# Neighbourhood attention in a two-layer diffusion trunk: turning the context keys' and context queries' probabilities by DMA instead of on TensorE, with half-precision values

## The chip, the cores and the metric

One core of one Trainium2 chip runs the whole program. The metric is device microseconds of one execution (us); lower is better. A core has five engines with a queue each: TensorE (PE, matmuls and transposes), VectorE (DVE), ScalarE (ACT), GpSimd (POOL) and SyncE (SP, which here only issues DMAs). Each engine takes its own instructions strictly in order.

## What is computed

Two layers of a trunk with 512 latent tokens (an 8 x 64 grid) and 256 context tokens, width 1024, 8 heads of 64. Each layer has two token mixers in parallel; the change touches the first, neighbourhood attention (below "NA"); the second is grouped-query attention ("GQ").

```python
s_win = einsum('bchd,bicjhd->bhcij', qr, kw) * scale + bias      # an 8 x 16 window of latent keys
s_ctx = einsum('bchd,blhd->bhcl', qr, kc) * scale                # all 256 context keys
p = softmax(concatenate([s_win, s_ctx]))
out = einsum(p_win, vw) + einsum(p_ctx, vc)                      # for the latent queries
c_a_att = _attend(cqa, cka, cva)      # layer 0 only: context queries read the context keys
```

The latent order is grid column by grid column, so that the window of 128 queries lies in 256 consecutive keys.

## The kernel before

**Stages.** Each layer runs one after the other: projections of K, V and Q for NA (line 433 to 435 are the three matmuls of every projection: a high and a low part of the activation against a high and a low part of the weight, each in fp32r), then the NA stage, then the projections of GQ, the GQ stage, and the merge with the output projection. While an attention stage runs, `pipeline` hands TensorE pieces of other projections as filling (the gates and z paths, tiles `psf` and `psx`), so that it has work while probabilities are made. Their weights come over SP's queue as `raw`, are rounded on ACT (`whi`) and the rest is taken on POOL or DVE (`wlo`).

**One head of the NA stage.** `na_scores` makes four tiles of 128 queries x 512 scores: for tile 0 the two edge groups of 64 queries, for tiles 1 to 3 128 inner queries; columns 0 to 255 are neighbours, columns 256 to 511 the 256 context keys. For each tile TensorE makes the scores in PSUM (`pss`); DVE adds the bias and takes the maximum (line 958, `p<-pss,bint` or `bedg`); ACT takes the exponential with its row sum (line 961); DVE inverts the sum (line 762); then the tile is multiplied with it, on DVE (line 765) for tiles 0 and 2 and on POOL (lines 767 and 768) for tiles 1 and 3 (`NA_POOL`). In layer 0 `ctx_scores` adds one tile for the 256 context queries.

`na_values` comes one head later (`pipeline` calls the scores of head h before the values of head h - 1). A value matmul needs the probabilities with the keys on the partitions, so each 128 x 128 block is turned first: `transpose_split` transposes four blocks on TensorE into one PSUM tile (`pst`, lines 777 and 779), ACT rounds it to fp32r (`pth`, line 785), DVE takes the rest (`ptl`, line 786). There are four such groups per head: two for the context keys (`k` = 0, 1: eight transposes, then lines 981 and 982 with 512 columns) and two for the neighbours (eight transposes, then lines 986 to 992 with 192 and 256 columns). In layer 0 `ctx_values` has one more group of four for the context queries (lines 905 and 906, 256 columns). The values themselves are four 64-column pieces per head (high, low, low, high, in fp32r), so that one matmul gives the product with the high part in one half of the partitions and the one with the low part in the other; `head_out` adds the halves and multiplies with the z path.

**GQ already turns by DMA.** There `turned` (lines 799 to 804) rounds the probabilities to fp16 on ACT (`h`, line 802), takes the rest in fp16 on POOL or DVE (line 803) and issues one `dma_start_transpose` on SP's queue (line 804), 12 blocks of 128 x 128 for a tile of 768 keys. Its values are fp16 pairs, scaled by one factor so that they fit.

**What sets the order.** The program is written head by head; a scheduler then places each engine's instructions, so an engine's queue can hold instructions of two heads and of filling mixed. Tiles come from pools with a fixed number of buffers: eight `p` (seven in layer 0), two `pth` and two `ptl`, three `raw`, eight `whi` and `wlo`, one `bint` and one `bedg` for the bias of a head. In layer 0 half of the adaLN gate's dot products (`gate_steps((0,), ...)`: line 295 on DVE, 16 of them, with eight weight tiles `rawb`) is spread over heads 4 to 7 of the NA stage.

Of the kernel before, what the change touches and what calls it, by code (L numbers as in the profile page):

```python
# [7 lines left out]
F32 = mybir.dt.float32  # L8
# [17 lines left out]
NP_NA = (7, 8)  # L26
# [3 lines left out]
NT_NA = 2  # L30
P_LOG = 9.7
V_UP = 2.0 ** 14
NA_POOL = (1, 3)
# [37 lines left out]
def hybrid_kernel(es: ExitStack, tc, x, ctx, cvec, w_ada, w_ada0, small, gvec, w_in, w_o_a, w_o_b, w_out,  # L71
# [482 lines left out]
    def split_v(ps, hi, lo, hi_src=None):  # L554
        S.copy(R(hi), ps)
        V.tensor_tensor(R(lo), ps, hi, ALU.subtract)

    def evac_va(dsts):
        def f(t, ps):
            d = dsts[t // 3].rearrange("p (t n) -> p t n", t=3)[:, t % 3, :]  # L560
            d = d.rearrange("p (r q d) -> p r q d", q=4, d=64)
            s = ps.rearrange("p (r e d) -> p r e d", e=2, d=64)
            hi, lo = d[:, :, 0:4:3, :], d[:, :, 1:3, :]
            split_v(s, hi, lo)
        return f
# [18 lines left out]
    def layer(l, hx, nxt, start):  # L584
# [144 lines left out]
        va = [big("va0"), big("va1")]  # L729
        w = load_w(W, C_AV, 512, KT, mix_lo)  # L730
        for t in range(6):
            tok_proj(w, 512, a_hx, t, evac_va(va))
            if first:
                if t == 0:
                    for ts in AKG[1:]:
                        evac_ak(ts)
                hp["lag"] = max(2, hp["lag"] - (t > 0))
            if t > 2:
                run(bg, per_bg)
# [9 lines left out]
        for t in range(qt):  # L749
            tok_proj(w, 512, a_hx, t, evac_na(qav, True, gq, YB if first else 4))  # L750
            run(bg, per_bg)
# [7 lines left out]
        if True:  # L759
            def softmax_tail(p, n, r, pieces, eng=None):  # L760

                V.reciprocal(r, r)
                for i, (c0, c1) in enumerate(pieces):
                    if eng is None:
                        V.tensor_scalar(p[:, c0:c1], p[:, c0:c1], r[:, i:i + 1], 0.5, ALU.mult, ALU.mult)
                    else:
                        G.tensor_scalar(r[:, i:i + 1], r[:, i:i + 1], 0.5, None, ALU.mult)
                        G.tensor_tensor(p[:, c0:c1], p[:, c0:c1],
                                        r[:, i:i + 1].to_broadcast([128, c1 - c0]), ALU.mult)

            def transpose_split(blocks, n0=0, n1=512):
# [8 lines left out]
                if att["spare"]:  # L780
                    hi, lo = R(p_tile()[:, 0:512]), R(p_tile()[:, 0:512])
                else:
                    hi = att["p"].tile([128, 512], F32R, tag="pth", name=nm("pth"), bufs=att["nt"])
                    lo = att["p"].tile([128, 512], F32R, tag="ptl", name=nm("ptl"), bufs=att["nt"])
                S.copy(hi[:, n0:n1], pt[:, n0:n1])
                V.tensor_tensor(lo[:, n0:n1], pt[:, n0:n1], F(hi[:, n0:n1]), ALU.subtract)
                return hi, lo

            def head_out(po, e, dst, eng=None):
# [5 lines left out]
                S.copy(a, po[o:o + 64, :n])  # L795
                V.tensor_tensor(a, po[m:m + 64, :n], a, ALU.add)
                (eng or G).tensor_tensor(dst, dst, a, ALU.mult)

            def turned(p, n, out, eng):

                h = att["p"].tile([128, 2, n], F16, tag="h", name=nm("h"), bufs=att["nh"])
                S.copy(h[:, 0], p[:, :n])  # L802
                eng.tensor_tensor(h[:, 1], p[:, :n], h[:, 0], ALU.subtract)  # L803
                nc.sync.dma_start_transpose(out, h.rearrange("p a n -> p (a n)"))
# [9 lines left out]

            def shrink(v, s, mx, row):

                V.tensor_reduce(mx[:, 0:1], v, AX, ALU.max)
                V.tensor_reduce(mx[:, 1:2], v, AX, ALU.min, negate=True)
                V.tensor_tensor(mx[:, 0:1], mx[:, 0:1], mx[:, 1:2], ALU.max)
                pt = psw(512, "t")  # L820
                T.transpose(pt[0:1, 0:128], mx[:, 0:1], ident)
                V.tensor_reduce(row[:, 0:1], pt[0:1, 0:128], AX, ALU.max)
                T.matmul(pt[:, 128:129], row[:, 0:1].to_broadcast([1, 128]), ident[0:1, 0:1], start=True, stop=True)
                V.tensor_scalar(s[:, 1:2], pt[:, 128:129], 1.0e-30, 1.0 / V_UP, ALU.max, ALU.mult)
                V.reciprocal(s[:, 0:1], s[:, 1:2])
                V.tensor_scalar(s[:, 1:2], s[:, 1:2], 0.5, None, ALU.mult)
# [40 lines left out]
            def ctx_scores(q, kh, kl, ct=None):  # L867
# [7 lines left out]
                if ct is not None:  # L875
# [6 lines left out]
                if ct is not None:  # L882
                    turned(p, 512, ct.rearrange("p a i k n -> p (a i k) n"), G)
                    return ct, r
                softmax_tail(p, 512, r, [(0, 256), (256, 512)])
                return p

            def ctx_values(p, vsl, dst, e, back=None):
                if back is not None:
                    ct, r = p  # L890
                    ps = psw(512, "v")
                    po = ps[:, 0:256]
                    divide(ps[:, 256:512], r, e, dst, back)
                    for k in range(2):
                        for a in range(2):
                            T.matmul(po.rearrange("p (i n) -> p i n", i=2), vsl(4 + k), ct[:, a, :, k, :],
                                     start=k + a == 0, stop=k + a == 2)
                    head_out(po, e, dst)
                    return
                hi, lo = transpose_split(  # L900
# [599 lines left out]
```

## Time and profile before

| what | us |
|---|---|
| median of 3 runs (1125.44 to 1126.06) | 1125.91 |
| the profiled execution | 1127.56 |
| its span, first to last instruction | 1125.6 |
| NA stage of layer 0, from the span's start | 149.5 to 305.2 |
| NA stage of layer 1 | 771.4 to 881.7 |
| GQ stage of layer 0 | 382 to 550 |
| GQ stage of layer 1 | 938 to 1061 |

The stages' limits are read from the first and last matmul of their lines. In a row of groups, "x35 | 19.7, 585" means 35 instructions, 19.7 us of busy time in all, 585 ns for one on average; what follows the second bar is the time that the engine was idle just before them, and who ended it. Matmuls are pipelined: the time of one reaches from its start to the end of its result, while the next has started long before. What one costs is therefore read from the distance of two starts in the timeline, not from its own duration.

### The profile page before, as it was taken

Reading aid. Unit: us, or ns where it says so; the run is one execution under the profiler, and the core shown is the slowest. Engines: PE = TensorE matmul, PEld = TensorE weight load, DVE = VectorE, ACT = ScalarE, POOL = GpSimd, SP = SyncE. Lnnn points to the kernel's source line nnn. Section 1 sums busy time; section 2 is a strip of 40 time slices with the busy share of each in tenths; the row PEclk is TensorE's granted clock in tenths of the full one; section 3 lists DMA queues with packets and bytes.
Section 4 is the critical chain, followed back from the end, with each engine's and each line's share of the span. In section 5 each row is a group of like instructions: output and inputs, shape, how many; then the busy total and the mean of one; then the engine's idle time right before and its main releaser. Section 6 shows DMA issues by size and latency. Waiting matters only on the chain.

```text
span 1125.6 us, 16862 instructions
## 1 busy us (share of the span) xinstructions
PE 1093.3 (97%) x5826; PEld 905.3 (80%) x5826; DVE 774.7 (69%) x1492; ACT 579.0 (51%) x1154; POOL 490.6 (44%) x405
## 2 busy tenths in 40 slices
PE   8999999999999999979999999999999999999998
PEld 5688888888998877757788888888888987776677
DVE  4666788897466477776577785458878765677473
ACT  6453266665433576755330284326666446776431
POOL 1054254654247144454521545235554563563531
PEclk9999999999999999989999999999999999999999
DMA  9454322242351488869633532553333236989742
GB/s 373 143 172 140 114 63 66 73 136 89 93 168 38 123 201 185 185 172 269 173 108 125 183 129 72 142 174 92 100 107 116 59 105 172 188 224 239 197 145 80
DMA packets 192222, 161.29 MB, mean 143 GB/s; under 512 B 116364, under 2 KB 158088, under 8 KB 190472
## 3 DMA queue, kind: packets, MB, share of 16 engines
q1 hardware_dynamic: 184800, 145.82, 46.8%
q0 software_dynamic: 2368, 7.87, 2.1%
q10 hardware_dynamic: 4968, 6.53, 1.7%
q8 instruction: 46, 0.75, 0.3%
q14 instruction: 40, 0.33, 0.1%
HBM read 115.58 MB, written 17.32 MB: 118 GB/s over the span
## 4 chain that ended last, share of the span: by engine, by line
PE 38%; issue 4%; DVE 3%; DMA 3%; POOL 2%; ACT 1%; SPq 1%; POOLq 0%; ACTq 0%
PE psx L435 6%; PE psx L433 6%; PE psx L434 6%; PE psf L433 4%; PE psf L434 4%; PE psf L435 4%; PE pss L955 1%; PE pss L861 1%; POOL wlo L406 1%; PE pss L862 1%; PE pst L779 1%; PE pst L1148 1%; DMA raw<-in_w_o_a_dram 1%; PE pst L1149 1%; DMA raw<-in_w_in_dram 1%
## 5 line engine op out<-in xcount | busy, mean ns | idle before, releaser
L420 POOL TENSOR_TENSOR wlo<-raw,whi 128x512 fp32r<-128x512 f32 x70 | 97.9, 1405 | 106.1 <-ACT whi L418 70.4
L433 PE MATMUL psf<-hx,whi 128*128 128x512 f32 (+1 forms) x360 | 138.0, 383 | 3.2 <-ACT zt L614 2.4
L435 PE MATMUL psf<-hx,wlo 128*128 128x512 f32 (+1 forms) x360 | 135.8, 377 | 0.0
L434 PE MATMUL psf<-hx,whi 128*128 128x512 f32 (+1 forms) x360 | 135.1, 375 | 0.0
L433 PE MATMUL psx<-whi,hx 128*128 128x512 f32 (+1 forms) x328 | 120.8, 372 | 0.0
L434 PE MATMUL psx<-wlo,hx 128*128 128x512 f32 (+1 forms) x328 | 119.6, 366 | 0.0
L435 PE MATMUL psx<-whi,hx 128*128 128x512 f32 (+1 forms) x328 | 119.5, 365 | 0.0
L418 ACT CAST whi<-raw 128x512 fp32r<-128x512 f32 x136 | 82.3, 620 | 64.0 <-DMA raw<-in_w_in_dram 35.3
L406 POOL TENSOR_TENSOR wlo<-raw,whi 128x512 fp32r<-128x512 f32 x40 | 61.2, 1535 | 122.1 <-ACT whi L403 80.1
L803 POOL TENSOR_TENSOR h<-p,h 128x768 f16<-128x768 f32 (+1 forms) x40 | 65.7, 1644 | 96.4 <-ACT h L802 72.0
L403 ACT CAST whi<-raw 128x512 fp32r<-128x512 f32 x88 | 54.1, 623 | 99.2 <-PE psx L435 34.2
L420 DVE TENSOR_TENSOR wlo<-raw,whi 128x512 fp32r<-128x512 f32 x66 | 73.6, 1115 | 30.6 <-ACT whi L418 29.0
L504 POOL TENSOR_TENSOR ss<-ss,ehalf 128x8 f32<-128x8 f32 (+2 forms) x40 | 62.5, 1566 | 72.9 <-DVE ss L501 72.8
L433 PEld LDWEIGHTS psf<-hx,whi 128*128 128x128 f32 x360 | 67.9, 188 | 15.4 <-ACT zt L614 3.7
L435 PEld LDWEIGHTS psf<-hx,wlo 128*128 128x128 f32 x360 | 67.8, 188 | 11.6
L1131 DVE CUSTOM_DVE_ANT_0 p<-pss,vb 128x768 f32<-128x768 f32 x64 | 60.3, 953 | 23.6 <-PE pss L862 21.1
L434 PEld LDWEIGHTS psf<-hx,whi 128*128 128x128 f32 x360 | 67.9, 189 | 10.3
L1132 ACT ACTIVATE p<-pss,mx 128x768 f32<-128x768 f32 x64 | 57.6, 900 | 34.7 <-DVE mx L1131 33.7
L435 PEld LDWEIGHTS psx<-whi,hx 128*128 128x128 f32 x328 | 61.9, 189 | 10.0
L434 PEld LDWEIGHTS psx<-wlo,hx 128*128 128x128 f32 x328 | 62.0, 189 | 9.2
L433 PEld LDWEIGHTS psx<-whi,hx 128*128 128x128 f32 x328 | 61.8, 189 | 8.9
L435 PE MATMUL psx<-hx,wlo 128*128 128x256 f32 (+1 forms) x208 | 68.0, 327 | 0.0
(362 smaller groups left out, 3095.8 us busy)
## 6 DMA issues: line engine op xcount, KB each, us to landing
raw<-in_w_in_dram SPq DMA_DIRECT2D x168, 256.0 KB, 2.9
rawb<-in_w_ada_dram SPq DMA_DIRECT2D x48, 256.0 KB, 2.8
raw<-in_w_out_dram SPq DMA_DIRECT2D x32, 256.0 KB, 2.9
tg<-gs SPq DMA_DIRECT2D x4, 1536.0 KB, 6.8
rawx<-in_w_ada_dram SPq DMA_DIRECT2D x4, 1024.0 KB, 9.8
rawy<-in_w_ada_dram SPq DMA_DIRECT2D x4, 1024.0 KB, 9.5
gs<-zt ACTq DMA_DIRECT2D x16, 256.0 KB, 2.0
raw<-in_w_o_a_dram SPq DMA_DIRECT2D x16, 256.0 KB, 3.4
```

What stands on the lines that cost most here:

```text
L403: S.copy(hi[:, :n], raw[:, :n])
L406: e.tensor_tensor(lo[:, :n], raw[:, :n], F(hi[:, :n]), ALU.subtract)
L418: S.copy(hi, raw)
L420: lo_eng(i).tensor_tensor(lo, raw, F(hi), ALU.subtract)
L433: T.matmul(ps, lhs[0], rhs[0], start=first, stop=False)
L434: T.matmul(ps, lhs[0], rhs[1], start=False, stop=False)
L435: T.matmul(ps, lhs[1], rhs[0], start=False, stop=last)
L504: G.tensor_tensor(ss, ss, ehalf[:, :n], ALU.pow)
L779: T.transpose(pt[:, c0:c0 + 128], src, ident)
L803: eng.tensor_tensor(h[:, 1], p[:, :n], h[:, 0], ALU.subtract)
L1131: V.tensor_tensor_reduce(p, pss, lift, -1.0, 3e38, ALU.add, ALU.min, mx[:, 0:1])
L1132: S.activation(p, pss, AF.Exp, bias=mx[:, 0:1], accum_out=r[:, i:i + 1])
```

## The change

1. **Context keys.** In `na_scores` columns 256 to 511 of each of the four tiles go through `turned`: ACT rounds 128 x 256 to fp16, POOL takes the rest, and DMA transposes on SP's queue put four blocks into `ht`, a tile in SBUF (two halves, used by even and odd heads). Tile 0 is split over two DMAs of 64 queries, because its halves belong at both ends of the 512 queries. `na_values` reads `ht` directly; the two groups of TensorE transposes with their ACT and DVE passes go.
2. **Context queries** (layer 0): the tile of 128 x 512 goes the same way with one DMA of eight blocks; one group of transposes goes.
3. **Neighbours** stay with `transpose_split`, but its two parts are now fp16.
4. **Values** of NA become fp16 pairs: each token tile is copied out, `size` takes its absolute maximum (ACT and DVE), `split_va` finds one factor for all (`shrink`: one transpose, one one-column matmul) and `halves` makes high and low. The probabilities are lifted by 2^14 (`P_UP`), `head_out` takes the factor back. GQ's values use the same helpers, with two pieces instead of three.
5. **Multiplication with the inverse sum** for tiles 1 and 3: on ACT instead of POOL (`NA_ACT`).
6. **Gate dots** of half 0: from NA of layer 0 to the projections of GQ of layer 0.
7. **Buffers**: eight `p` in both layers, four `h`, one `hc`; `pth` and `ptl` become one fp16 tile `pt`.

```diff
-NA_POOL = (1, 3)
+NA_ACT = (1, 3)
+P_UP = 2.0 ** 14
...
+            if t == 0:
+                split_va()
...
-                    if eng is None:
-                        V.tensor_scalar(p[:, c0:c1], p[:, c0:c1], r[:, i:i + 1], 0.5, ALU.mult, ALU.mult)
+                    if on_act:
+                        S.activation(p[:, c0:c1], p[:, c0:c1], AF.Copy, scale=r[:, i:i + 1])
                     else:
-                        G.tensor_scalar(r[:, i:i + 1], r[:, i:i + 1], 0.5, None, ALU.mult)
-                        G.tensor_tensor(p[:, c0:c1], p[:, c0:c1],
-                                        r[:, i:i + 1].to_broadcast([128, c1 - c0]), ALU.mult)
+                        V.tensor_scalar(p[:, c0:c1], p[:, c0:c1], r[:, i:i + 1], P_UP, ALU.mult, ALU.mult)
...
-                nc.sync.dma_start_transpose(out, h.rearrange("p a n -> p (a n)"))
+                for o, n0, n1 in out:
+                    nc.sync.dma_start_transpose(o, h[n0:n1].rearrange("p a n -> p (a n)"))
...
-                    softmax_tail(p, 512, r[:, 0:1], [(0, 512)], G if i in NA_POOL else None)
+                    softmax_tail(p, 512, r[:, 0:1], [(0, 512)], i in NA_ACT)
+                    at = [(0, 64, 0), (448, 512, 64)] if i == 0 else [(128 * i - 64, 128 * i + 64, 0)]
+                    turned(p[:, 256:512], 256, [(ht[:, :, a:b], n, n + b - a) for a, b, n in at], G)
...
                 for k in range(2):
-                    c0 = 256 + 128 * k
-                    hi, lo = transpose_split(
-                        [(pe[:, c0:c0 + 128], None)]
-                        + [(pp[:, c0:c0 + 128], 64 + 128 * i) for i, pp in enumerate((p0, p1, p2))])
-                    T.matmul(po, vsl(4 + k), hi, start=k == 0, stop=False)
-                    T.matmul(po, vsl(4 + k), lo, start=False, stop=False)
+                    for a in range(2):
+                        T.matmul(po, vsl(4 + k), ht[:, 2 * a + k, :], start=k + a == 0, stop=False)
...
-            bg = gate_steps((0,), att["p"]) if first else []
+            bg = []
...
-            bg = []
+            bg = gate_steps((0,), hp["p"]) if first else []
```

**TensorE, NA of layer 1.** Before, this stands in TensorE's queue around the values of head 4 (`psv_8685`) and the context keys of head 5 (`pst_8844` and `pst_8855`, each four transposes of tiles `p`):

```order
L991 MATMUL psv_8685<-ptl_8727,va_1485_7303 128x256
L992 MATMUL psv_8685<-ptl_8727,va_1486_7304 128x192
L777 MATMUL pst_8844<-ident,p_8646 128x2x64
L779 MATMUL pst_8844<-ident,p_8656 128x128
L779 MATMUL pst_8844<-ident,p_8667 128x128
L779 MATMUL pst_8844<-ident,p_8677 128x128
L777 MATMUL pst_8855<-ident,p_8646 128x2x64
L779 MATMUL pst_8855<-ident,p_8656 128x128
L779 MATMUL pst_8855<-ident,p_8667 128x128
L779 MATMUL pst_8855<-ident,p_8677 128x128
L955 MATMUL pss_8969<-kh_7883,qs_8951 128x512
```

In the changed kernel, the values of head 4 (`psv_8687`) read the context keys' probabilities from `ht` with no transposes ahead of them; these rows are the last of their four matmuls and the first of the neighbours' (`pt`), each weight load a row of its own:

```order
L996 LDWEIGHTS va_7261
L996 MATMUL psv_8687<-ht_7859,va_7261 128x512
L1000 LDWEIGHTS va_7261
L1000 MATMUL psv_8687<-pt_8697,va_7261 128x192
L1001 LDWEIGHTS va_7261
L1001 MATMUL psv_8687<-pt_8697,va_7261 128x256
```

Eight transposes per head have left this queue; what the matmuls wait for is now a DMA's landing instead of ACT's and DVE's passes over a PSUM tile.

**SP, NA of layer 1.** Before, SP's queue holds the weights of the filling (`raw`), the bias of each head (`bint`, `bedg`) and stores of the z path (`zs`, `gs`):

```order
L618 DMA gs_83<-zt_8787 128x512
L415 DMA raw_8942<-in_w_in_dram 128x2x256
L935 DMA bedg_7875<-in_bias_edge_dram 64x128 x2
L415 DMA raw_9245<-in_w_in_dram 128x2x256
L618 DMA gs_83<-zt_8921 128x512
L415 DMA raw_9251<-in_w_in_dram 128x2x256
```

In the changed kernel, halfway through the stage, the turns of heads 3 and 4 (`h_8366` is the last tile of head 3, `h_8477` to `h_8522` are head 4's) stand between them:

```order
L840 DMA_TRANSPOSE ht_7859<-h_8366 128x4x128
L840 DMA_TRANSPOSE ht_7859<-h_8477 128x4x64 x2
L840 DMA_TRANSPOSE ht_7859<-h_8493 128x4x128
L840 DMA_TRANSPOSE ht_7859<-h_8507 128x4x128
L947 DMA bint_7853<-in_bias_int_dram 128x256
L417 DMA raw_8921<-in_w_in_dram 128x2x256
L417 DMA raw_9201<-in_w_in_dram 128x2x256
L417 DMA raw_9207<-in_w_in_dram 128x2x256
L949 DMA bedg_7854<-in_bias_edge_dram 64x128
L840 DMA_TRANSPOSE ht_7859<-h_8522 128x4x128
```

The bias of the next head and the next weights are now queued behind turns, and head 4's last turn behind three weight loads.

**ACT, NA of layer 1.** Before, one stretch of the stage's end (line 785 is the pass over four turned blocks, 961 the exponential):

```order
L795 COPY ho_8734<-psv_8685 64x512
L785 CAST pth_8849<-pst_8844 128x512
L785 CAST pth_8860<-pst_8855 128x512
L403 CAST whi_9283<-raw_9281 128x512
L403 CAST whi_9289<-raw_9287 128x512
L614 ACTIVATE zt_9216<-psf_9191 128x512
L785 CAST pth_8871<-pst_8866 128x448
```

In the changed kernel (line 835 rounds the context keys' half to fp16, 793 is the multiplication for tiles 1 and 3, 978 the exponential, 811 the pass over turned neighbours):

```order
L835 CAST h_8948<-p_8941 128x256
L793 ACTIVATE p_8956<-p_8956,r_8959 128x512
L623 ACTIVATE zt_9083<-psf_9058 128x512
L978 ACTIVATE p_8985,r_8988<-p_8985,mx_8986 128x512
L835 CAST h_8964<-p_8956 128x256
L835 CAST h_8978<-p_8971 128x256
L420 CAST whi_9221<-raw_9219 128x512
L825 ACTIVATE ho_8871<-psv_8842,vsa_7262 64x512
```

Two passes of 512 columns per head have become four of 256 and two multiplications of 512.

174 lines of the change are left out of this document (92 added, 82 removed).

## The prediction

> **What bounds the kernel now.** I read the page first: does one engine fill the span?
>
> ```profile
> span 1125.6 us, 16862 instructions
> PE 1093.3 (97%) x5826; PEld 905.3 (80%) x5826; DVE 774.7 (69%) x1492; ACT 579.0 (51%) x1154; POOL 490.6 (44%) x405
> ```
>
> TensorE does, and the next engine, DVE, stands at 69%. An average hides stages, so the second view is the busy time of each engine by stage, over windows that begin and end with matmuls of a stage's lines:
>
> ```profile
> core 0: us, PE busy (x) PEld busy (x) DVE busy (x) ACT busy (x) POOL busy (x), PEclk, DMA share, GB/s
> 63.00:149.50 86.50, 86.50 (x423) 72.34 (x422) 60.50 (x119) 35.52 (x62) 37.37 (x21) 1.00 0.43 125
> 149.50:305.20 155.70, 155.70 (x976) 139.03 (x975) 123.15 (x272) 93.81 (x212) 75.47 (x74) 1.00 0.28 87
> 305.20:382.00 76.80, 76.80 (x451) 67.31 (x450) 42.72 (x76) 30.58 (x63) 38.67 (x31) 1.00 0.35 111
> 382.00:550.00 168.00, 153.11 (x850) 122.05 (x849) 115.96 (x207) 105.09 (x203) 75.97 (x54) 0.97 0.80 187
> 771.40:881.70 110.30, 108.81 (x596) 93.10 (x595) 94.02 (x186) 72.46 (x151) 57.41 (x57) 1.00 0.33 102
> 938.00:1061.00 123.00, 117.86 (x556) 88.31 (x554) 81.00 (x129) 83.59 (x149) 65.87 (x44) 1.00 0.91 208
> ```
>
> The second and fifth rows are the NA stages of layers 0 and 1, where the change works. TensorE is busy for 155.70 of 155.70 us and for 108.81 of 110.30 us (98.65%). Here an instruction taken from TensorE shortens the stage, as long as no other engine or queue becomes late. The fourth and sixth rows are the GQ stages, which already turn by DMA: TensorE's share is 91.1% and 95.8%, the DMA share 0.80 and 0.91 instead of about 0.3. They are my yardstick for what such a stage loses. The first and third rows hold the projections ahead of the two stages of layer 0, where the value split and the gate dots land. The profiled execution took 1127.56 us, 1.65 above the median of 1125.91; I make the sum on the profiled one and take its difference off the median.
>
> **The change, part by part.**
>
> **TensorE loses transposes.** Per head eight for the context keys, and in layer 0 four for the context queries: 8 x 12 = 96 in NA of layer 0, 8 x 8 = 64 in layer 1, 160 in all. What one costs I read from starts on TensorE's timeline:
>
> ```profile
> 825.67 0.27 PE L777 MATMUL pst<-ident,p 128*128 128x128 f32 x1
> 825.78 0.49 PE L779 MATMUL pst<-ident,p 128*128 128x128 f32 x3
> 826.03 0.47 PE L434 MATMUL psf<-hx,whi 128*128 128x512 f32 x1
> 826.34 0.39 PE L435 MATMUL psf<-hx,wlo 128*128 128x512 f32 x1
> ```
>
> Four transposes and one matmul of 512 columns take 826.34 - 825.67 = 0.67 us; the matmul alone takes 0.23 (below), so a transpose is 0.44 / 4 = 0.11 us. That is 10.6 us in layer 0 and 7.0 in layer 1, 17.6 together. Each transpose by itself is listed longer, in the first row of the groups:
>
> ```profile
> L779 PE MATMUL pst<-ident,p 128*128 128x128 f32 x212 | 35.3, 272 | 0.0
> L785 ACT CAST pth<-pst 128x512 fp32r<-128x512 f32 x35 | 19.7, 585 | 6.5 <-PE pst L779 4.8 <-PE psv L905 1.4
> L786 DVE TENSOR_TENSOR ptl<-pst,pth 128x512 fp32r<-128x512 f32 x35 | 23.4, 682 | 3.1 <-ACT pth L785 2.9
> L768 POOL TENSOR_TENSOR p<-p,r 128x512 f32<-128x512 f32 x32 | 35.0, 1093 | 2.7
> L767 POOL TENSOR_SCALAR r<-r 128x1 f32<-128x1 f32 x32 | 10.8, 338 | 54.3 <-DVE r L762 31.8 <-ACT za L614 5.3 <-ACT p L880 4.4
> L541 ACT ACTIVATE ka<-pst,gk 128x512 f32<-128x512 f32 x12 | 8.1, 687 | 0.2
> L382 ACT CAST hx<-yT 128x256 fp32r<-128x256 f32 x21 | 8.0, 406 | 8.7 <-DVE yT L380 8.7
> L803 POOL TENSOR_TENSOR h<-p,h 128x768 f16<-128x768 f32 x32 | 56.0, 1750 | 89.7 <-ACT h L802 70.1 <-issue 13.8 <-PE psf L435 5.1
> L803 POOL TENSOR_TENSOR h<-p,h 128x512 f16<-128x512 f32 x8 | 9.8, 1219 | 6.7 <-issue 4.7 <-ACT h L802 1.9
> L295 DVE CUSTOM_DVE_ANT_0 rawb<-rawb,cb 128x512 f32<-128x512 f32 x56 | 41.3, 740 | 10.0 <-DMA rawb<-in_w_ada_dram 8.4 <-DMA cb<-cd 1.1
> ```
>
> Its 272 ns run to the end of the result, with the next started long before; I keep 0.11. The Trainium skill ("TensorE: Matmul & The Clock Gate", "Part 4: PE-mode transpose") gives about 275 ns for a transpose in a kernel, which agrees with the listed 272. If that were its price in the queue, 160 of them would give an estimate of 44 us and a time near 1084; the starts 0.11 us apart speak against it.
>
> **Half-precision values.** Three short stretches of TensorE's timeline compare the two formats:
>
> ```profile
> 816.86 0.25 PE L986 MATMUL psv<-ptl,va 128*128 128x192 f32 x1
> ...
> 817.29 0.31 PE L991 MATMUL psv<-ptl,va 128*128 128x256 f32 x1
> ...
> 819.10 0.39 PE L434 MATMUL psx<-hx,whi 128*128 128x512 f32 x1
> ...
> 820.92 0.39 PE L955 MATMUL pss<-kh,qs 128*128 128x512 f32 x1
> ...
> 962.06 0.38 PE L1148 MATMUL pst<-ht,vb 128*128 128x512 f16 x1
> ...
> 963.79 0.38 PE L1148 MATMUL pst<-ht,vb 128*128 128x512 f16 x1
> ```
>
> Eight matmuls of 512 columns start over 1.82 us in fp32r (0.2275 each) and over 1.73 in fp16 (0.216). The context keys' four per head (two key blocks, two parts), 64 in both layers, save 64 x 0.0115 = 0.7 us. The neighbours' short ones start four in 0.43 us; their 896 columns at fp16's 0.216 / 512 make 0.38, so 32 such fours save 1.6. With 0.3 for the context queries that is 2.6: 1.5 in layer 0, 1.1 in layer 1. Taken from TensorE: **12.1 us in layer 0, 8.1 in layer 1**. Added are one transpose and one matmul of one column per layer for the values' factor, 4 x 0.11 = 0.4 us in all.
>
> **ACT** (72.5 busy of 110.3 in layer 1) loses two rounding passes per head (16 x 0.585 = 9.4), gains 16 multiplications like the scaled copy of line 541 (16 x 0.687 = 11.0) and 32 roundings of 256 columns like line 382 (32 x 0.406 = 13.0): 87 us of a stage of about 105. In layer 0: 93.8 - 14.0 + 11.0 + 13.0 + 5 for the context queries, 109 of about 146. **DVE** loses 16 x 0.682 = 10.9 in layer 1 (83 left) and in layer 0 16.4 and the 16 gate dots (95 left). **POOL** loses 16 x (1.093 + 0.338) = 22.9 and gains 32 subtractions of 256 columns; line 803 at 512 and 768 columns gives 2.07 ns a column, so an estimated 0.69 us each, 22: as before in layer 1, and 8 x 1.22 more in layer 0 (84). All of it lies beside TensorE; none of the engines passes 84% of its stage, but ACT at 83% in layer 1 is the fullest, and is what I charge for below.
>
> **The turns** move to SP's queue and DMA:
>
> ```profile
> ht<-h SPq DMA_TRANSPOSE x64, 4.2
> ct<-h SPq DMA_TRANSPOSE x4, 3.7
> 403.42 1.57 SPq L804 DMA_TRANSPOSE ht<-h  x1
> ...
> 406.53 3.96 SPq L804 DMA_TRANSPOSE ht<-h  x2
> ```
>
> From issue to landing a turn of 12 blocks takes 4.2 us, one of 8 blocks 3.7, so 0.125 us a block and an estimated 3.2 us for the new turns of four. SP's queue is held 1.6 us by one and 2.0 by each of two. Per head there are now four subtractions and five turns (tile 0 goes in two), in a head period of 110.3 / 8 = 13.8 us. The values of a head are read one head later, so 3.2 us of latency are covered several times. DMA: half of the 64 turns, of 12 blocks each, lift GQ of layer 1 to a share of 0.91 over 123 us, against 0.33 in NA; (0.91 - 0.33) x 123 us / 384 blocks is 0.19 us a block, and 128 blocks add 24 us to NA of layer 1, 192 add 36 in layer 0: shares of about 0.57 and 0.54, under GQ's 0.91. What can come late is ACT: it rounds into one of four `h`, and one is held for 0.41 + 0.69 + up to 2.0 + 3.2 = 6.3 us, 1.6 us per piece with four buffers, where 13.8 / 4 = 3.4 us are to be had. The next head's bias and weights are queued behind turns on SP, each of which waits for POOL; if POOL is late, weights come late and TensorE's filling with them. That loss I cannot compute from before; its ends are nothing (NA keeps its shares) and what GQ loses.
>
> **Work moved.** Sixteen gate dots (16 x 0.740 = 11.8 us of DVE) go to the projections of GQ in layer 0: 42.7 + 11.8 = 54.5 of 76.8 us, covered by TensorE; 11.8 is the price without cover. Their eight `rawb` loads stand there ahead of some of the query weights on SP, at a DMA share of 0.35. The value split adds per layer six absolute values on ACT and six maxima on DVE, and three larger passes on each, an estimated 8 us on each at the 0.585 and 0.682 of the rows, into a stretch where ACT has 35.5 and DVE 60.5 of 86.5: nothing, up to 8 without cover.
>
> **The sum.** TensorE's own work in NA falls to 155.7 - 12.1 = 143.6 and 108.8 - 8.1 = 100.7. I don't let it stay at 100% in layer 0: with turns it gets layer 1's old 98.65%, so 145.6; layer 1, with the fuller ACT and the bias behind turns, gets GQ's 95.8%, so 105.1. The stages shorten by 10.1 and 5.2; with 0.4 added, **14.9 us**: 1112.7 for the profiled execution, 1111 for the median.
>
> **The rivals.**
>
> *Full gain.* The shares stay 100% and 98.65%: -12.1 - 8.1 / 0.9865 + 0.4 = -19.9, 1106. For it speaks that all turned tiles have a head's time to land.
>
> *Both stages like GQ of layer 1* (95.8%): 149.9 and 105.1, -5.8 - 5.2 + 0.4 = -10.6, 1115. ACT waiting for `h`, or weights behind turns, would do it.
>
> *Both like GQ of layer 0* (91.1%): 157.6 and 110.5, +1.9 + 0.2 + 0.4 = +2.5, 1128.5: the gain is eaten by waits. Against it: GQ's low share goes with a DMA share of 0.80 and with 12 blocks per tile, three times those of NA.
>
> *Slower: the turns run one after another.* If each turn had to land before the next started, a head would need 5 x 3.2 = 16 us, and 19.7 with the context queries' 3.7: 128 us in layer 1 and 157.6 in layer 0, +17.7 + 1.9 + 0.4 = +20, 1146. It decides from a turn period of 110.3 / 40 = 2.76 us. Against it: the two issues that follow 406.53 hold SP for 1.98 us each, while one takes 4.2 to land, so turns overlap. The Trainium skill ("VectorE: DVE Perf Modes", "The three transpose paths") speaks for it: it gives 1309 ns for one 128 x 128 block by DMA against 390 on TensorE, and its "Rules for kernel authors" choose TensorE where PSUM will do. By 1309 ns a block, layer 0's 24 blocks would take an estimated 31 us a head, 251 in the stage; this trace's 4.2 us for 12 blocks, 0.35 a block with the latency in it, disagrees.
>
> **How the numbers follow.** Forecast 1111: 0.40. Full gain 0.25. Like GQ of layer 1 0.15. Like GQ of layer 0 0.08, which straddles the bound. Turns in series, or another loss of that size, 0.12. About 0.2% (2.3 us) is what a measurement of this kernel can tell from no change. Faster by more: 0.40 + 0.25 + 0.15 = 0.80; within: 0.05 of the 0.08; slower: 0.03 + 0.12 = 0.15. The range that holds the first three, with 3 us below the full gain (transposes and short matmuls of up to 0.13 us instead of 0.11) and up to 8 above the third for an uncovered split, is 1103 to 1123, with 0.20 left outside.
>
> **What would show it.** NA of layer 0 should take about 146 us and of layer 1 about 105, with 160 fewer transposes, and GQ as before. If ACT's casts to `h` wait for DMA, or matmuls for `raw` or `whi`, the GQ cases hold. If the turns' landing time grows well above 4 us and TensorE waits for `ht`, they run in series. If the projections of GQ in layer 0 take more than 77 us, the gate dots lost their cover. The prediction is wrong if TensorE stays as busy in shorter NA stages but the other stages grow.

## The result and the profile after

The changed kernel takes 1123.88 us (median of 20 runs) against 1126.29 for the kernel before (median of 20): ratio 0.9976, 95% interval 0.9968 to 0.9984. It is faster, by 0.24% instead of the 1.3% that was forecast, and the time lies 0.9 us above the upper end of the range.

The page of the changed kernel begins so (the profiled execution took 1125.00 us):

```profile
span 1122.9 us, 16871 instructions
PE 1079.4 (96%) x5672; PEld 876.5 (78%) x5672; DVE 761.7 (68%) x1496; ACT 616.7 (55%) x1236; POOL 497.0 (44%) x413
```

TensorE's busy time fell by 14 us, the span by 2.7. By stage (windows of the changed kernel: the projections ahead of NA in layer 0, NA of layer 0, the projections ahead of GQ in layer 0, and then layer 1 from its first projection to the start of GQ):

```profile
core 0: us, PE busy (x) PEld busy (x) DVE busy (x) ACT busy (x) POOL busy (x), PEclk, DMA share, GB/s
62.50:150.60 88.10, 87.69 (x426) 72.58 (x425) 65.97 (x127) 41.86 (x71) 38.39 (x21) 1.00 0.39 110
150.60:302.70 152.10, 148.34 (x893) 126.22 (x892) 108.53 (x239) 109.06 (x246) 81.14 (x83) 0.98 0.52 127
302.70:379.50 76.80, 76.03 (x439) 66.14 (x439) 50.21 (x100) 29.66 (x60) 37.34 (x29) 1.00 0.43 132
665.00:936.70 271.70, 264.99 (x1339) 215.41 (x1338) 179.90 (x362) 161.37 (x333) 134.89 (x112) 1.00 0.45 126
```

The same two stretches of the kernel before, NA of layer 0 up to the first projection behind it and layer 1:

```profile
149.50:306.80 157.30, 157.30 (x989) 140.62 (x988) 124.35 (x274) 95.13 (x214) 76.46 (x74) 1.00 0.28 87
666.30:938.20 271.90, 269.96 (x1400) 228.27 (x1399) 189.42 (x356) 143.49 (x292) 133.86 (x112) 1.00 0.36 110
```

In layer 1 I read NA and the projections around it as one: in the changed kernel's queue 37 more matmuls of filling stand ahead of the first scores (109 instead of 72), so the stage's own limits have moved. NA of layer 0 is 5.2 us shorter, layer 1 is unchanged to 0.2 us, although TensorE has 61 instructions less in it. TensorE, once gapless, now waits. In NA of layer 1 TensorE waits for 6.6 us in all (five of the eight kinds of wait there, each with total, times and longest):

```profile
PE pss L972 <- DVE mx L975: 1.8, 3, 0.8
PE pss L996 <- DMA ht<-h: 1.3, 1, 1.3
PE pst L805 <- ACT p L793: 0.8, 1, 0.8
PE psv L996 <- DVE pt L812: 0.7, 1, 0.7
PE psv L996 <- DMA ht<-h: 0.6, 1, 0.6
```

Where does such a wait come from? Follow one back. These rows are from the timelines of SP, then DVE, then TensorE in NA of layer 1; the second number is how long the instruction holds its engine, and the bracket is what ended the idle time before it:

```profile
847.32 1.24 SPq L840 DMA_TRANSPOSE ht<-h  x1
848.65 0.53 SPq L627 DMA_DIRECT2D gs<-zt  x1
849.28 2.72 SPq L840 DMA_TRANSPOSE ht<-h  x2
852.09 0.91 SPq L947 DMA_DIRECT2D bint<-in_bias_int_dram  x1
853.06 0.48 SPq L949 DMA_DIRECT2D bedg<-in_bias_edge_dram  x1
854.78 3.86 SPq L840 DMA_TRANSPOSE ht<-h  x3
```

```profile
850.92 0.15 DVE L790 TENSOR_SCALAR r<-r 128x1 f32<-128x1 f32 x1
855.47 0.69 DVE L975 CUSTOM_DVE_ANT_0 p<-pss,bedg 128x512 f32<-128x512 f32 x1 [4.40 <-DMA bedg<-in_bias_edge_dram]
```

```profile
856.22 0.50 PE L972 MATMUL pss<-kh,qs 128*128 128x512 f32 x1 [0.62 <-DVE mx L975]
```

A half of the next head's edge bias is issued at 853.06, behind turns that held SP from 847.3 on (the other half went out at 844.19, ahead of them). DVE stands still for 4.40 us until it has landed, and the next scores wait for the PSUM that DVE has yet to read. TensorE's filling covers most of it, 0.62 us shows. The page's busy shares say nothing of SP, since DMA-issuing instructions aren't counted; its timeline has to be added up. In NA of layer 1 (779.5 to 877.6) 40 turns hold it 48.9 us, 21 loads of bias 13.7, 20 of weights 8.2, 9 stores 4.2: 75 of 98 us, 0.76. Before it was 24 of 110, 0.22.

### The profile page after: what moved, and what is told of

Read it like the earlier page. It is cut to its first block, busy times and chain, and to the rows that moved or that the text cites. A ratio compares the mean times of both kernels' runs of the same rounds, so it can differ in the third digit from the quotient of the medians.

```text
span 1122.9 us, 16871 instructions
## 1 busy us (share of the span) xinstructions
PE 1079.4 (96%) x5672; PEld 876.5 (78%) x5672; DVE 761.7 (68%) x1496; ACT 616.7 (55%) x1236; POOL 497.0 (44%) x413
## 5 line engine op out<-in xcount | busy, mean ns | idle before, releaser
L836 POOL TENSOR_TENSOR h<-p,h 128x256 f16<-128x256 f32 (+2 forms) x104 | 112.5, 1090 | 144.3 <-ACT h L835 106.7
L422 DVE TENSOR_TENSOR wlo<-raw,whi 128x512 fp32r<-128x512 f32 x66 | 69.5, 1054 | 36.5 <-ACT whi L420 35.0
L835 ACT CAST h<-p 128x256 f16<-128x256 f32 (+2 forms) x136 | 81.3, 616 | 11.4 <-DMA ct<-h 5.1
L437 PEld LDWEIGHTS psx<-whi,hx 128*128 128x128 f32 x328 | 62.0, 189 | 10.3
L435 PE MATMUL psx<-hx,whi 128*128 128x256 f32 (+1 forms) x208 | 69.0, 332 | 0.0
```

The lines of the kernel that those rows point to most:

```text
L422: lo_eng(i).tensor_tensor(lo, raw, F(hi), ALU.subtract)
L435: T.matmul(ps, lhs[0], rhs[0], start=first, stop=False)
L437: T.matmul(ps, lhs[1], rhs[0], start=False, stop=last)
```

## The experiments

All ratios are to the kernel before, timed beside the run on the same chip, with the 95% interval. The windows and waits of a run are of one execution, which can lie some us from the median (r9's took 1114.04 us, its median is 1116.47; r7's 1117.68, its median 1115.29).

| run | ratio | interval |
|---|---|---|
| the change | 0.9976 | 0.9968 to 0.9984 |
| r1 context turned on TensorE | 1.0051 | 1.0039 to 1.0064 |
| r2 no bias loads after head 0 | 0.9878 | 0.9864 to 0.9891 |
| r3 fixed factor of the values | 0.9976 | 0.9967 to 0.9986 |
| r4 before, gate dots moved | 1.0021 | 1.0012 to 1.0030 |
| r5 before, no bias loads after head 0 | 1.0030 | 1.0020 to 1.0041 |
| r6 two bias buffers | 0.9967 | 0.9954 to 0.9980 |
| r7 bias on POOL's queue | 0.9904 | 0.9890 to 0.9917 |
| r8 multiplication on POOL | 1.0071 | 1.0057 to 1.0084 |
| r9 turns in pairs | 0.9912 | 0.9896 to 0.9928 |
| r10 turns in halves | 1.0244 | 1.0225 to 1.0264 |
| r11 pairs, bias on POOL's queue | 0.9951 | 0.9932 to 0.9969 |
| r12 as r11, dots back in NA | 0.9971 | 0.9957 to 0.9985 |
| r13 pairs, two bias buffers | 0.9966 | 0.9954 to 0.9978 |
| r14 pairs, no bias loads after head 0 | 0.9868 | 0.9849 to 0.9887 |
| r15 bias on POOL's queue, two buffers | 0.9983 | 0.9970 to 0.9997 |

The theories: **W**, the turns took the work off TensorE as forecast and new waits gave most of it back; **Q**, the loads of bias come late because of their place behind the turns in SP's queue, which would be W's waits; **S**, which took Q's place after r6, SP's queue is held by the turns, and whatever stands behind them comes late; **F**, filling used up ahead of NA is missing in it; **V**, the value split, ACT's multiplication or the gate dots ate the gain; **N**, the transposes had been nearly free.

**r1: the turns undone.** In `na_values` and `ctx_values` of the changed kernel the blocks go through `transpose_split` again:

```diff
-                    turned(p[:, 256:512], 256, [(ht[:, :, a:b], n, n + b - a) for a, b, n in at], G)
...
+                    hi, lo = transpose_split(
+                        [(pe[:, c0:c0 + 128], None)]
+                        + [(pp[:, c0:c0 + 128], 64 + 128 * i) for i, pp in enumerate((p0, p1, p2))])
+                    T.matmul(po, vsl(4 + k), hi, start=k == 0, stop=False)
+                    T.matmul(po, vsl(4 + k), lo, start=False, stop=False)
```

> The changed kernel with the context keys and context queries turned on TensorE again (fp16 values, ACT's multiplication, moved gate dots stay). Theory W (the turns took about 17 us of work off TensorE, and new waits in the NA stages gave about 11 of it back): TensorE gets its 160 transposes back and the named waits of the NA stages (11 us) go, so 1127 to 1132. Rival V (the gain of the turns is whole, and the value split, ACT's multiplication or the gate dots ate it): the full 17 us are lost, 1139 to 1143. Rival N (the transposes had been nearly free): 1122 to 1125.

1133.30 us, 1.0051: 0.0075, 8.4 us, slower than the change. Its windows of NA of layer 0 and of layer 1:

```profile
150.30:306.20 155.90, 155.90 (x985) 132.37 (x984) 114.90 (x255) 106.96 (x229) 50.23 (x42) 1.00 0.24 75
668.20:945.00 276.80, 271.39 (x1403) 222.09 (x1402) 188.23 (x377) 159.61 (x317) 111.62 (x80) 1.00 0.36 108
```

The turns gain 8.4 us net as they stand. TensorE is busy without a gap again in NA of layer 0, at 155.9 us. W's direction holds; 1133.30 lies 1.3 us above its range, and farther from V's and N's (the kernel before took 1127.52 beside this run). One thing is left over: r1 is 5.7 us slower than the kernel before, so without the turns the other parts of the change lose time, and layer 1 is 4.9 us longer than before (276.8 against 271.9). r4 finds 2.4 us of a loss in the gate dots of layer 0; what lengthens layer 1 no run takes apart.

**r2 and r5: no bias loads**, in the changed kernel and in the one before; all heads then use the bias of head 0, so these two runs, and r14, show a time but not the whole result:

```diff
-                load_bias(h)
+                if h == 0:
+                    load_bias(h)
```

> The changed kernel, but the bias is loaded for head 0 of each layer only and used for all heads (part of the computation is changed: every head has the bias of head 0). Theory Q (bias loads queued behind turns on SP make DVE, and with it the scores, late): DVE's 7.2 us of waits for bias in NA of layer 1 go, TensorE's waits for the maximum with them, 1118 to 1121. Rival F (it is the missing filling, the bias only fills the idle time): 1123 to 1124.

> The control for r2: the kernel before with the bias loaded for head 0 of each layer only and used for all heads (part of the computation is changed: every head has the bias of head 0). Theory Q (the loads cost only because they are queued behind turns): within 0.2% of before, ratio 0.998 to 1.002. Rival L (the bias loads cost about 11 us in any version, by their traffic or their waits): ratio about 0.990.

The changed kernel gains 0.0098, 11 us, and at 1113.56 more than Q expected; the kernel before gains nothing (it lost 0.3%, just outside Q's 0.2%, in GQ, which the edit doesn't touch). So it is not the loads, but the loads beside the turns. r2's windows of the same two stretches:

```profile
150.40:297.70 147.30, 145.58 (x892) 124.41 (x891) 102.74 (x239) 108.29 (x246) 83.11 (x83) 1.00 0.50 122
659.60:926.00 266.40, 263.00 (x1339) 215.90 (x1338) 173.89 (x362) 161.34 (x332) 135.07 (x112) 1.00 0.45 123
```

They are 10.0 and 5.5 us shorter than before the change: the forecast's 10.1 and 5.2, though with the bias loads gone.

**r3: a fixed factor.** No maxima, and the filling back where it was:

```diff
-            size(ps, vab[:, 512 * t:512 * t + 512], vmx[:, t:t + 1])
...
-            V.tensor_reduce(vmx[:, 6:7], vmx[:, 0:6], AX, ALU.max)
-            shrink(vmx[:, 6:7], vsa, vsa[0:1, 2:3], 0.5 / P_UP)
+            V.memset(vsa[:, 0:1], 64.0)
+            V.memset(vsa[:, 1:2], 0.5 / P_UP / 64.0)
```

> The changed kernel with a fixed factor for NA's values, without the passes that take the maximum and the two small TensorE instructions (the factor isn't taken from the data). In TensorE's queue 72 instead of 109 filling matmuls then stand between the last projection of the queries and the first scores of layer 1, as before the change. Theory F (filling spent ahead of NA of layer 1 is missing in it): its waits of 6.6 us fall to 1 or 2, 1118 to 1120. Rival Q or others (the waits come from queues that filling doesn't cure): 1122 to 1124, for the 0.4 us of TensorE work and a wait of 0.6 in the projections alone.

0.9976, as the change; 1124.72 us is not F's 1118 to 1120. F falls: with the filling in its place layer 1 takes 273.3 us instead of 271.7. The value split costs nothing that shows.

**r4: the gate dots alone**, moved in the kernel before (`bg = gate_steps(...)` of half 0 from NA to the stage behind it).

> The kernel before with only the gate dots of half 0 moved to the projections of GQ in layer 0. Theory C (they lost their cover there): 1 us slower, 1127 to 1128. Rival: free, or a relief for DVE in NA of layer 0, 1125 to 1126.5.

2.4 us slower, more than either expected. The projections of GQ in layer 0 took 78.5 us (75.8 before), NA of layer 0 gained nothing:

```profile
306.20:384.70 78.50, 76.28 (x441) 66.27 (x440) 51.94 (x107) 29.25 (x61) 38.23 (x30) 1.00 0.46 140
```

**r6, r7: the bias away from the turns.** r6 has two tiles each for `bint` and `bedg` and calls `load_bias(h + 1)` at the start of head h; r7 only this, in both loads:

```diff
-                nc.sync.dma_start(bint[:, 0:256], bias_int[l, h])
+                nc.gpsimd.dma_start(bint[:, 0:256], bias_int[l, h])
```

> The changed kernel with two buffers each for the inner and the edge bias, and the loads of head h + 1 given at the start of head h, so that they stand about a head earlier in SP's queue; all loads and turns stay. Theory Q (the place in SP's queue is what costs): nearly all of r2's gain, ratio 0.987 to 0.990. Rival T (it is the time that 48 loads hold SP or the DMA engines): 0.995 to 0.998, as the change itself.

> The changed kernel with the bias loads issued by POOL instead of SP, still one buffer each. Theory Q (turns ahead of them on SP): the loads pass the turns, but each now stands in POOL's order behind subtractions, so half to all of r2's gain, ratio 0.988 to 0.993. Rival B (the single buffer, which is free only after the last tile of the head before, is what makes them late): 0.996 to 0.999.

r7 gains 0.0072, 8 us, over the change, as Q expected; r6 gains 1 us, and here Q, with its 0.987 to 0.990, was wrong: 0.9967 is what rival T expected, for which the time that the loads hold SP or the DMA engines counts, not their place. An earlier place in the same queue doesn't help; leaving the queue does. r7's windows:

```profile
151.90:299.20 147.30, 145.75 (x892) 124.38 (x891) 105.84 (x239) 108.69 (x246) 94.12 (x104) 1.00 0.53 131
661.00:930.10 269.10, 263.12 (x1339) 215.64 (x1338) 177.72 (x361) 161.39 (x332) 146.97 (x136) 1.00 0.47 127
```

In r6 the bias no longer makes DVE wait in NA of layer 1 at all, and layer 1 takes 271.6 us all the same, so the late bias alone is not the cause. Of r7's gain 4.8 us lie in NA of layer 0 (147.3 instead of 152.1) and 2.6 in layer 1, about half of the 5.0 us by which layer 1 fell short of the forecast.

**r8: the multiplication back on POOL.**

```diff
-                        S.activation(p[:, c0:c1], p[:, c0:c1], AF.Copy, scale=r[:, i:i + 1])
+                        G.tensor_scalar(r[:, i:i + 1], r[:, i:i + 1], P_UP, None, ALU.mult)
+                        G.tensor_tensor(p[:, c0:c1], p[:, c0:c1],
+                                        r[:, i:i + 1].to_broadcast([128, c1 - c0]), ALU.mult)
```

> The changed kernel with the multiplication of tiles 1 and 3 back on POOL (two instructions of 0.34 and 1.09 us as before) instead of ACT. Theory A (ACT, the fullest engine beside TensorE, is not what sets NA's end; POOL then feeds the turns later): the same or slower, ratio 0.997 to 1.003. Rival (ACT's 11 us more per layer are part of the lost gain): 0.992 to 0.996.

1.0071: 10.7 us slower than the change, more than expected. POOL makes the fp16 remainders that every turn waits for; with the multiplication before them they come later, and TensorE's waits for `ht` in NA of layer 1 grow from 1.9 us (the two `ht` rows above) to

```profile
PE psv L996 <- DMA ht<-h: 3.7, 2, 3.1
```

That is 1.8 of the 6.7 us by which layer 1 grew (278.4 instead of 271.7). TensorE's waits for DVE's maxima (`mx`) grew there as well, from 2.4 to 4.9 us, and its granted clock fell to 0.98. So ACT's 11 us per layer more, which the prediction charged as the fullest engine, are worth their price; that late turns are the whole reason is not shown.

**r9, r10: fewer and more turns for the same blocks.** r9 puts two tiles into one `h` and turns them at once (`turn_pair`, 16 turns of eight blocks per layer), r10 turns every tile in two halves:

```diff
+                for i, p in enumerate(ps):
+                    S.copy(h[:, i, 0], p[:, 256:512])
+                    G.tensor_tensor(h[:, i, 1], p[:, 256:512], h[:, i, 0], ALU.subtract)
+                nc.sync.dma_start_transpose(out, h.rearrange("p t a n -> p (t a n)"))
```

```diff
-                    at = [(0, 64, 0), (448, 512, 64)] if i == 0 else [(128 * i - 64, 128 * i + 64, 0)]
+                    at = [(0, 64, 0), (448, 512, 64)] if i == 0 else [(128 * i - 64, 128 * i, 0), (128 * i, 128 * i + 64, 64)]
```

> The changed kernel with two tiles per turn: 16 turns of eight blocks instead of 40 of four (or half of four) per layer, the same blocks in all; the edge tile's halves are taken apart by two matmuls (128 and 384 columns instead of 512). Three `h` of twice the size. Bias stays on SP. Theory S (SP's queue is held 1.2 us by each turn, whatever its size, and is 0.76 full in NA of layer 1): SP gets back 24 x 1.2 = 29 us per layer, ratio 0.987 to 0.991. Rival B (DMA blocks and their landing set the pace): no gain or a loss, as a pair lands later, 0.997 to 1.002.

> The changed kernel with every tile turned in two DMAs of 64 queries, as tile 0 is: 64 turns per layer instead of 40, the same blocks. Theory S: SP needs 24 x 1.2 = 29 us more per layer, 104 of the 98 us that NA of layer 1 takes, so SP becomes the bound: that stage grows by 10 to 25 us, ratio 1.010 to 1.035 in all. Rival B: ratio 0.996 to 1.000, as the change.

0.9912 and 1.0244: S expected 0.987 to 0.991 and 1.010 to 1.035, so r9 lies at the edge and r10 inside; the rival expected neither. First r9's windows of NA of layer 0 and of layer 1, then r10's:

```profile
149.10:296.50 147.40, 146.06 (x924) 125.90 (x923) 99.60 (x239) 107.40 (x246) 84.28 (x83) 1.00 0.53 131
658.30:927.50 269.20, 263.11 (x1371) 217.90 (x1370) 175.10 (x361) 161.99 (x332) 137.36 (x112) 1.00 0.47 127
```

```profile
150.40:304.80 154.40, 148.34 (x892) 124.83 (x891) 105.23 (x239) 108.06 (x246) 82.19 (x83) 0.99 0.50 125
663.60:965.40 301.80, 274.71 (x1340) 222.34 (x1340) 174.86 (x365) 163.77 (x336) 139.83 (x113) 0.95 0.41 114
```

r10 moves the same bytes; its DMA share is lower, not higher. Layer 1 grew by 30.1 us, more than the 10 to 25 that S expected. 24 more turns of 1.22 us are 29.3, but that the two agree is partly chance: 20.4 of the 30.1 are waits of TensorE (27.1 us of the stage instead of 6.7), and 9.7 are a longer busy time at a granted clock of 0.95. Nor is SP full on average: from NA's first scores, at 779.7, to 907 it is held for 102 of 127 us, 0.80. What it has is stretches without a gap, such as this one, behind which the loads of bias and weights wait:

```profile
841.78 28.29 SPq L840 DMA_TRANSPOSE ht<-h  x22
```

Layer 0, where a head has 19 us instead of 12, grew by 2.3 against the change and by 7 against r7 and r9.

**r11 to r15: do the cures add?** r11 joins r7 and r9. r12 adds the gate dots in NA of layer 0, with two `h` and seven `p`. r13 is r9 with r6's buffers and two `h` instead of three, r14 r9 without bias loads, r15 r7 with r6's buffers.

> r9 with the bias loads on POOL's queue as in r7. Theory S: SP falls to about 0.35 in NA; little is left to gain beyond r7 and r9, ratio 0.985 to 0.990. Rival (turns and bias are separate causes that add): 0.981 to 0.985.

> r11 with the gate dots back in NA of layer 0, for which `h` has two buffers instead of three, shared with the context queries' tile, and `p` seven in layer 0. Theory C (the dots cost 1 to 2.5 us in the projections of GQ, where r4 lost 2.4): 1 to 2.5 us faster than r11. Rival (DVE, the fewer buffers or the eight weight loads make NA of layer 0 longer by as much): as r11 or slower.

> r9 (two tiles per turn, bias on SP) with two buffers for the bias as in r6, and two `h` instead of three. Theory S (SP's hold by turns is what made everything behind it late): r9 has taken it away, so 0.989 to 0.992, as r9. Rival M (a late bias is a second cause of its own, which hid behind the first in r6): 0.984 to 0.988.

> r9 with the bias loaded for head 0 only (part of the computation is changed: every head has the bias of head 0). Theory S: turns and bias loads are one cause, the hold of SP's queue, so that without the loads the pairs gain nothing beyond r2: 0.986 to 0.989. Rival M: the two gains add, 0.979 to 0.984.

> r7 (single turns, bias on POOL's queue) with two buffers for the bias. Theory S: as r7, 0.989 to 0.992, since the loads are off SP either way. Rival M: up to r2's 0.986 to 0.988, if the 3 us between r7 and r2 are loads that wait for their one buffer in POOL's order.

r14 equals r2 (the intervals overlap over most of their length): without the bias loads the pairs gain nothing more. Turns and bias loads thus act as one cause, as S says. But S had expected r11 at 0.985 to 0.990 and r13 and r15 at 0.989 to 0.992, and missed all three, as the rivals did: r11 and r15 are slower than r7, r11 and r13 slower than r9, by 0.4% to 0.8%. SP is not held for longer there: the share of NA of layer 1 for which it is held is 0.35 in r11, 0.42 in r13 and 0.65 in r15, against 0.44 in r9 and 0.67 in r7. So S is not the whole account. Layer 1 of r11, r13 and r15:

```profile
663.40:934.30 270.90, 266.17 (x1370) 219.69 (x1370) 180.68 (x361) 161.51 (x333) 146.93 (x136) 0.99 0.46 126
661.30:934.20 272.90, 265.92 (x1371) 218.65 (x1370) 182.34 (x366) 161.58 (x333) 136.09 (x112) 0.99 0.46 125
664.00:937.50 273.50, 265.12 (x1339) 217.46 (x1338) 185.70 (x365) 160.65 (x332) 149.82 (x136) 0.99 0.45 125
```

With at most five instructions more, DVE is busy for 180.68 to 185.70 us instead of 175.10 (r9) and 177.72 (r7), and TensorE, at a clock of 0.99 instead of 1.00, 2.0 to 3.1 us longer for the same work. The last section tells of both, DVE beside POOL and the clock after a wait; that they are the reason here, no run shows. Each edit also makes the scheduler place all queues anew, and r5 moved by 0.3% for no reason of its own, so differences of that size between single edits aren't explained here.

Against r11, r12's dots' stage is 2.0 us shorter (75.9 against 77.9) and its NA of layer 0 2.4 longer (153.3 against 150.9): moving the dots back gained nothing, as the rival expected, but the fewer buffers stand in that figure too. r7 and r9 are the fastest kernels that compute the whole result, 0.72% and 0.64% faster than the change and 0.9% faster than before.

## Why the prediction was wrong, point by point

**TensorE's work: right.** Forecast were 12.1 and 8.1 us less. Where SP has more room (r7), TensorE's busy time is 145.75 instead of 157.30 us in NA of layer 0 and 263.12 instead of 269.96 in layer 1: 11.6 and 6.8 less. Between r1 and r7 lie 0.0147, 16.6 us, for the 160 transposes that were priced at 17.6; between r1 and r2 19.5. N is out. So is the estimate of 44 us from the 275 ns of the Trainium skill ("TensorE: Matmul & The Clock Gate", "Part 4: PE-mode transpose"): the starts 0.11 us apart told the price.

**ACT, DVE, POOL: sizes right, one meaning wrong.** ACT's 109.06 us in NA of layer 0 were forecast as 109, POOL's 81.14 as 84. DVE has 108.53 instead of 95. Part of that are instructions that are drawn out (last section): r9 has as many instructions of DVE there, 239, and 99.60 us. And 2.4 us are 16 scalings of `r` (line 790), which came to DVE with the multiplication on ACT and which the sum left out. I charged ACT as what comes late; r8 shows that its load saves 10.7 us, and part of the reason is that POOL feeds the turns.

**The turns: this step failed in layer 1.** The DMA was better than I reckoned: a turn of four blocks lands 2.4 us after issue, not 3.2, and the DMA share in NA of layer 0 is 0.52, forecast 0.54.

```profile
ht<-h SPq DMA_TRANSPOSE x40, 2.4
```

The step had SP's hold in front of it ("SP's queue is held 1.6 us by one and 2.0 by each of two") and didn't add it up: 40 turns at even 1.6 us are 64 us of a stage of 105, on top of 24 that were there. Measured are 1.22 us per turn, 49 in all, and with the loads and stores SP is held for 0.76 of the stage. Instead the prediction asked whether turns come in time (they do, but for 1.9 us of waits in NA of layer 1) and said of what stands behind them: "That loss I cannot compute from before; its ends are nothing (NA keeps its shares) and what GQ loses". r10 shows what more turns cost, r9 and r7 that about half of what layer 1 lacks is to be had back (2.5 and 2.6 of 5.0 us), r2 that the forecast's stage times are met when the bias loads are gone. Why r11, r13 and r15 fall back stays open.

**The loss taken from GQ's shares: too small.** NA of layer 0 was to gain 10.1 us and gained 5.2, layer 1 was to gain 5.2 and gained 0.2: 9.9 us of the 12.2 that are missing (2.7 instead of 14.9). In layer 1 this is at least in part the queue. In layer 0 one event is large enough for all of it, a wait of 3.2 us and a slow clock behind it (last section); it isn't in r2, r6, r7 or r9, but in r3. SP's hold isn't what sets it apart: r6 holds SP in that stage for 86.0 us, the change for 85.1. The rows lead to DVE instead, and to a second step of the prediction that failed, "All of it lies beside TensorE": DVE was added up from durations that stand in the rows as means, and here two of its instructions took 3.87 and 3.31 us instead of 0.49 and 0.95, with a transpose of TensorE waiting behind them. r3 has the same two at 3.88 and 3.31 us; in r2, r6, r7 and r9 the longest such multiplication in that stage takes 2.02.

**Work moved: wrong for the dots, right for the split.** The dots were taken as hidden. Alone they cost 2.4 us (r4), in the changed kernel 1.0 in their stage (76.8 against 75.8). The split costs nothing (r3). The projections ahead of NA in layer 0 are 1.6 us longer (88.1 against 86.5), in r3 too (88.4), so it is not the maxima; what it is stays open.

**Rivals.** Turns one after another, at 1146, didn't come: they overlap. r10's 1153 shows where that rival was right in kind: a series can set the pace for a stretch, but it is a series of issues on SP, at 1.22 us each, not of landings at 3.2, and what counts is all that SP issues, not the turns alone.

## What to carry to other kernels

When work goes from an engine to a DMA, add up the queue that issues it, like an engine: so many instructions by the time that each holds the queue, plus what already stands there. A profile that counts no busy time for issuing shows that queue nowhere but in its timeline, and an early sign can be another engine waiting for a small load that has nothing to do with the change. Join small transfers into one issue, or give the loads that others wait for a queue of their own; test one cure at a time, for here two together were worse than either. And where an engine's busy time grows with the same instructions, look at what its neighbour does in the same microseconds.

## What the runs showed of the hardware

**In NA a turn's issue costs the same for half blocks as for eight.** On SP four half blocks (r10) hold it 1.23 us, four blocks 1.22, eight 1.25 (medians of their rows in NA). In GQ of the kernel before, where the DMA share is 0.80 and 0.91, twelve took 1.48 and 1.80 (medians of the two layers), and eight 1.73 (four turns of layer 0), so the size alone doesn't make it longer. A plain load of weights holds it 0.4.

**DVE is drawn out beside POOL.** In NA of layer 0 of the changed kernel, first DVE's rows, then POOL's in the same microseconds:

```profile
178.47 3.87 DVE L795 TENSOR_SCALAR p<-p,r 128x512 f32<-128x512 f32 x1
...
185.91 3.31 DVE L878 TENSOR_TENSOR qs<-qa,qs 64x768 fp32r<-64x768 f32 x1
189.25 0.49 DVE L795 TENSOR_SCALAR p<-p,r 128x512 f32<-128x512 f32 x1
```

```profile
178.10 1.58 POOL L827 TENSOR_TENSOR za<-za,ho 64x512 f32<-64x512 f32 x1 [3.00 <-DMA bedg<-in_bias_edge_dram]
179.66 1.16 POOL L836 TENSOR_TENSOR hc<-p,hc 128x512 f16<-128x512 f32 x1
180.78 1.27 POOL L422 TENSOR_TENSOR wlo<-raw,whi 128x512 fp32r<-128x512 f32 x1
```

The same multiplication takes 0.49 us at 189.25 and 3.87 at 178.47, where it ends 0.3 us after a row of three POOL instructions without a gap. All 32 rows of this multiplication in the trace say the same: the 13 with POOL idle take 0.48 to 0.49 us each, the 19 that overlap with POOL up to 3.87. The subtraction `wlo` of line 422 takes 0.67 to 0.69 in its 24 rows with POOL idle and up to 8.2 beside POOL, the subtraction `qs` of line 878 (64x768) 0.95 to 0.96 in seven rows with POOL idle and up to 3.31 beside it. Line 975, which reads the scores from PSUM, isn't drawn out: 0.67 to 0.69 in the 23 rows that lie beside POOL, 0.68 to 0.69 in the 14 alone. The Trainium skill ("GPSIMD Engine Reference", "1. Specifications") says that the two engines share their SBUF interfaces, with contention for some DVE instructions, among them those with two inputs in SBUF; the rows agree (`wlo` and `qs` have two, line 975 one), though no run here takes POOL away to prove it.

**A wait of 2 to 3 us can halve TensorE's clock for a while.** What follows behind the `qs` and the multiplication above, on TensorE's timeline, and then its windows (span, busy times, PEclk third from the end):

```profile
186.23 0.38 PE L803 MATMUL pst<-ident,p 128*128 128x128 f32 x2
189.80 0.48 PE L805 MATMUL pst<-ident,p 128*128 128x128 f32 x1 [3.19 <-DVE p L795]
```

```profile
186.00:190.60 4.60, 1.08 (x5) 0.57 (x4) 4.57 (x5) 4.53 (x13) 2.41 (x2) 0.84 0.14 26
190.60:194.00 3.40, 3.16 (x13) 1.74 (x12) 3.37 (x8) 2.21 (x5) 2.88 (x4) 0.50 0.51 155
194.00:198.00 4.00, 4.00 (x28) 3.96 (x27) 2.87 (x10) 3.69 (x9) 2.91 (x5) 0.76 0.74 188
```

The granted clock is 0.50 for 3.4 us and 0.76 over the next 4, about 0.5 x 3.4 + 0.24 x 4 = 2.7 us of work lost on top of the wait. From the three rows, the clock is at half from 189.1 to 195.9, 6.8 us. A shorter wait was enough in NA of layer 1 of r11 (from TensorE's timeline there):

```profile
817.75 0.66 PE L980 MATMUL pss<-kh,qs 128*128 128x512 f32 x1 [2.09 <-DVE mx L983]
...
818.63 0.63 PE L435 MATMUL psx<-hx,whi 128*128 128x512 f32 x1
819.05 0.63 PE L436 MATMUL psx<-hx,whi 128*128 128x512 f32 x1
...
821.96 0.39 PE L435 MATMUL psx<-hx,whi 128*128 128x512 f32 x1
822.18 0.39 PE L436 MATMUL psx<-hx,whi 128*128 128x512 f32 x1
```

After 2.09 us of waiting the granted clock is 0.50 from 817.9 to 821.3, 3.4 us, in which matmuls of 512 columns start 0.42 us apart instead of 0.22 behind it. Not every such wait does it: in NA of layer 0 of r15 one of 2.3 us passes with the clock at 1.00. The Trainium skill ("TensorE: Matmul & The Clock Gate", "Part 1: The HAM clock gate (the "warmup" mystery)") gives half clock after an idle window of about 3.4 us and full clock again after about 3.4 us of work. The half clock agrees, and so does its length in r11, while here it is twice that; but waits of 3.2 and 2.1 us, shorter than that window, were enough, and the measurement decides.
